# A joint product in three more pairs of units, and buffers handed out by hand, in a two-layer hybrid decoder trunk on one core

## The chip, the cores and the metric

The kernel runs on 1 core of a Trainium2 chip. The metric is the device time in microseconds; the median of 3 runs of the kernel before is 1880.92 us (1879.19 to 1881.81). Five engines work in the core, each through its own list of instructions in order: PE (TensorE) multiplies matrices into PSUM, DVE (VectorE) and ACT (ScalarE) do arithmetic on rows, POOL (GpSimd) here issues the DMAs that add into memory, and SP (SyncE) issues almost all other DMAs. 16 DMA engines carry the transfers.

## What is computed

One inference step of a decoder layer for 1024 prompt rows and 8 sample rows together (T = 1032 rows, width 1024). A projection feeds three branches: a convolution with a gated linear recurrence, windowed attention, and attention to a memory. Their results are gated, summed, projected, and normalised. Then comes the part that the change touches, the gated feed-forward block, here from the reference:

```python
h = layer_norm(ALPHA * x + merged @ w_out, ln1_g, ln1_b)
gt, up = jnp.split(h @ w_gate_up, 2, axis=-1)
h = layer_norm(ALPHA * h + (jax.nn.silu(gt) * up) @ w_down, ln2_g, ln2_b)
```

The hidden width is 2816, that is 22 blocks of 128 columns. All matrices are float32. The kernel keeps nearly full precision by writing each operand as a sum of a rounded high part and a low part (this is called a cut below: ACT copies the high part, DVE subtracts it to get the low part) and by making three matmuls per tile: high times high, high times low, low times high.

## The kernel before

**Seven products for eight.** A unit is two blocks of 128 output columns for all rows, that is a 2 x 2 arrangement of weight blocks times a 2 x 2 arrangement of row blocks. It is computed with seven block products instead of eight, numbered 0 to 6. Product i has a stationary operand made from the unit's weights (a sum or difference of quarters, `fast_quarter`, line 263 on) and a moving operand made once from the rows, `ts[p][i]`, for two quarters of the columns p = 0 and 1. One product is 2 (p) x 4 (k) x 3 = 24 matmuls of 128 x 128 by 128 x 258 (`fast_product`). `fast_step` (line 297) runs product i and then moves what is ready out of PSUM: bank b takes products 0, 2, 4 and 6 one on top of the other, so that its state must be read between them (copies p1s and u2s by ACT, the sum zb by DVE, a copy by ACT at the end); bank d takes 1 and 5; bank c takes 3. The outputs are two tiles of 128 x 1032, za and zb.

**The stages around the change.** Two gate blocks (f = 0 and 1) are made plainly. Then `gate_up_down` (line 1440) goes through a list of 28 units: 20 gate units f = 2 to 21 (gate column block f and up column block f), then 4 units of the first down part (rows of w_down for hidden blocks 0 to 7), then 4 of the second (blocks 8 to 15). The last six hidden blocks, 16 to 21, are multiplied plainly in `last_products`, where the second norm is also made. A gate unit ends in `FinishGate`: Silu of za times zb, stored to a scratch `f` in memory. A down unit ends in `FinishDown`: za and zb are added to the scratch `h` by DMAs of POOL.

**The joint product.** In the first nine pairs of gate units (u, v), the products 3 of both units use the same moving operand. They are made together with the same trick one level down (`second_quarter`, `second_step`, lines 1326 and 1350): seven half-size products called p0 (two of them), p1 (two), p4 (two) and p6 (one), 12 + 12 + 12 + 6 = 42 matmuls in place of 48. Their moving operands `t2` are made once, in `second_combos`, from tiles R of the normed rows. The tenth pair (f = 20, 21) and all down units are plain, with 7 x 24 matmuls a unit.

**The order.** The order of products is written out as a list. Three products ahead of PE the weights are cut (`quarter(*order[n + ahead])`). Side work is stepped on from the same loop: copies between memories, the means of the last weights (`weight_means`), the sums of hidden rows for the down parts (`down_sums`, which read `f`, add, and store to a scratch `t`) and the moving operands of the next part (`down_operand`: a load of 516 KB from `f` or `t` for each p, and a cut into the slots of an operand that is no longer needed). For the first down part, operand 0 is made in product 3 of the last but one gate unit, and operand i+1 in product i of the last one. A planner then puts each engine's instructions in order, by program order among those that it expects to be ready.

**Buffers.** Tiles of rows (`zt`, line 187) come from a pool of ten, sums of weights from a pool of four, raw weight tiles of 128 x 512 (256 KB) from a pool of six; the planner picks the slots. Raw weights of a unit are requested by `load` when product 1 of the unit before is issued; a pair with a joint product loads nine tiles, one of them twice.

Of the kernel before, what the change touches and what calls it, by code (L numbers as in the profile page):

```python
# [10 lines left out]
F32 = mybir.dt.float32  # L11
# [8 lines left out]
P = 128  # L20
# [40 lines left out]
class Builder:  # L61
# [124 lines left out]

    def zt(self, name):
        return self.z.tile([P, T], F32, tag="z", name=name, bufs=self.zbufs)
# [47 lines left out]
    def pair_load(self, u, st, src0, src1, other=None):  # L236

        h = D // 2
        raw = lambda j, e, src: self.half_raw(src[:, e * h:(e + 1) * h], h, f"ur{u}_{j}{e}")
        if other is not None:  # L240
            a11, a12, a21, a22 = (raw(j, e, src) for j, src in enumerate((src0, src1)) for e in range(2))
            st["second"] = raw(2, 1, other)
        else:
            a11, a21, a22, a12 = raw(0, 0, src0), raw(1, 0, src1), raw(1, 1, src1), raw(0, 1, src0)
        return {"raw": [[a11, a12], [a21, a22]], "u": u}
# [14 lines left out]

    def fast_quarter(self, st, i):

        nc, (a11, a12), u = self.nc, st["raw"][0], st["u"]
        a21, a22 = st["raw"][1] or (None, None)
        if i in (1, 2, 4, 5):
            src = st[2] if i == 5 and self.sum_bufs == 4 else self.w1.tile([P, D // 2], F32, tag="sum", name=f"us{u}_{i}",
                                                                          bufs=self.sum_bufs)
            a, b = {1: (a21, a22), 2: (st.get(1), a11), 4: (a11, a21), 5: (st.get(2), a12)}[i]
            nc.vector.tensor_add(src, a, b)
            st[i] = src  # L270
        else:
            src = {0: a11, 3: a12, 6: a22}[i]
        hi, lo = self.half_pair(f"u{u}_{i}")
        self.split(hi, lo, src)
        st["q", i] = hi, lo
# [21 lines left out]
    def fast_step(self, st, i, ts, finish):  # L297
# [9 lines left out]
        for p in range(2):  # L307
# [10 lines left out]
            if i in (0, 1, 2):  # L318
# [16 lines left out]
        if st.get("pd") is not None and i == 0:  # L335
            nc.vector.scalar_tensor_tensor(st["s", 0, 1], st["pd"]["p", 1], 1.0, st["s", 0, 1], op0=ALU.mult,
                                           op1=ALU.subtract)
# [864 lines left out]
    def out_proj(self, merged):  # L1202
        nc, io, ph = self.nc, self.io, self.ph
        h, self.R, self.norm, w = {}, {}, None, []
        for q in range(4):
            for kh in range(2):
                t = self.zt(f"R{q}{kh}")
                nc.sync.dma_start(t, io["xQ"][kh, q])
                self.R[q, kh] = t.rearrange("p (k n) -> p k n", k=4)
# [36 lines left out]
    def h_combos(self, h, ts):  # L1246
# [9 lines left out]
        for p in range(2):  # L1256
            b11, b21, b12, b22 = self.R[p, 0], self.R[p, 1], self.R[2 + p, 0], self.R[2 + p, 1]
            t1 = self.zt(f"ht1_{p}").rearrange("p (k n) -> p k n", k=4)
            tt(t1, b11, b12, ALU.subtract)
            keep(1, p, t1)  # L1260
            yield
# [6 lines left out]
            keep(6, p, b11)  # L1268
            yield

    def plain_gate_up(self, f, h, steps):
# [21 lines left out]
        nc.sync.dma_start(self.scr["f"][:, f, :], out)  # L1293

# [12 lines left out]
    def second_combos(self):  # L1307

        nc, tt = self.nc, self.nc.vector.tensor_tensor
        (b11, b21), (b12, b22) = ((self.R[p, 1][:, 0:2, :], self.R[p, 1][:, 2:4, :]) for p in range(2))  # L1310
# [12 lines left out]
        self.split(*self.t2[6], b21)  # L1323
        yield

    def second_quarter(self, su, sv, j):

        add, h = self.nc.vector.tensor_add, D // 4
        a, b = su["raw"][0][1], sv["second"]
# [4 lines left out]
        elif j == 1:  # L1334
            src, z = (self.w1.tile([P, D // 2], F32, tag="sum", name=f"us{su['u']}_p{e}", bufs=4) for e in range(2))
# [7 lines left out]
        else:  # L1343
            src, n = sv["raw"][0][1][:, hi], h
        wh, wl = self.half_pair(f"u{su['u']}_p{j}")
        self.split(wh[:, :n], wl[:, :n], src)
        for e, i in enumerate({0: (0, 3), 1: (1, 2), 4: (4, 5), 6: (6,)}[j]):
            su["w", i] = wh[:, e * h:(e + 1) * h], wl[:, e * h:(e + 1) * h]

    def second_step(self, su, sv, j, ts, fu):  # L1350

        nc, u = self.nc, su["u"]
        stt = nc.vector.scalar_tensor_tensor
        part = lambda p, e: tuple(a[:, 2 * e:2 * e + 2, :] for a in ts[p][3])
        quarter = lambda z, p: z[:, QN * p:QN * (p + 1)]
        if j == 0:
            su["p", 0], su["p", 3] = (self.bank("s", f"p{e}{u}")[:, :QN] for e in "bc")
            su["p", 1] = self.bank("o", f"pd{u}")[:, :QN]
            su["za"] = self.zt(f"za{u}")
        b, c, d = su["p", 0], su["p", 3], su["p", 1]  # L1360
        for i in {0: (0, 3), 1: (1, 2), 4: (4, 5), 6: (6,)}[j]:
# [10 lines left out]
            if i == 0:  # L1372
                stt(su["s", 0, 0], b, 1.0, su["s", 0, 0], op0=ALU.mult, op1=ALU.add)
            elif i == 3:
                stt(quarter(su["za"], 0), c, 1.0, su["s", 0, 0], op0=ALU.mult, op1=ALU.add)
# [637 lines left out]
```

## Time and profile before

| | before |
|---|---|
| median of 3 runs | 1880.92 us |
| the profiled execution | 1882.15 us |
| its span, first to last instruction | 1880.4 us |
| PE busy | 1861.4 us, 14670 matmuls |
| DVE busy | 1396.7 us, 2807 instructions |
| ACT busy | 1058.6 us, 2264 instructions |
| POOL busy | 125.0 us |
| DMA | 308.14 MB, mean 164 GB/s |
| granted PE clock, mean | 0.997 |

The stage with the list of 28 units runs from about 1237 us to about 1798 us of the span. Rows of instructions give the start, the duration, the engine, the line of the kernel, the operation, output and inputs by the program's names (`ufg_4h` is the high part of the cut weights of product 4 of a gate unit, `uf_4h` that of a down unit, `d04h` or `dth` a moving operand of a down part), and in brackets the idle time before and what ended it. A matmul's duration of 0.28 us covers its whole passage; successive ones start 0.12 us apart.

### The profile page before, as it was taken

The numbers are of one execution on the slowest core, as the hardware profiler recorded it, in microseconds if no ns is written. First come the engines' busy times: TensorE is split into PE (matmuls) and PEld (weight loads), VectorE is DVE, ScalarE is ACT, GpSimd is POOL, SyncE is SP. The second block draws the span as 40 slices with busy tenths as digits, with TensorE's granted clock in tenths as the row PEclk, the third lists the DMA queues.
The fourth block names the chain that finished last, engine by engine and source line by source line (L and its number), as shares of the span: only waits on it lengthen the run. The fifth ranks groups of instructions, "written<-read, shape, count | busy, mean of one in ns | idle before, by whom it ended". The sixth has DMA issues, their size and how long they took to land.

```text
span 1880.4 us, 37977 instructions
## 1 busy us (share of the span) xinstructions
PE 1861.4 (99%) x14670; PEld 1846.0 (98%) x14670; DVE 1396.7 (74%) x2807; ACT 1058.6 (56%) x2264; POOL 125.0 (7%) x187
## 2 busy tenths in 40 slices
PE   9999999999999999999999999999999999999998
PEld 9999999999999999999999999999999999999998
DVE  7878878888788757568787567786677667858486
ACT  6576676665666756568774234544444444635454
POOL 1001002110000000021210000000000000001100
PEclk9999999999999999999999999999999999999998
DMA  9535345447344368647535251224355345758872
GB/s 329 175 117 174 108 145 167 137 139 267 117 160 164 120 198 267 213 128 238 170 103 189 91 192 57 69 88 146 123 182 201 95 152 194 260 139 266 173 212 91
DMA packets 182213, 308.14 MB, mean 164 GB/s; under 512 B 19264, under 2 KB 97040, under 8 KB 182032
## 3 DMA queue, kind: packets, MB, share of 16 engines
q1 hardware_dynamic: 174928, 286.08, 45.9%
q0 software_dynamic: 4224, 14.78, 4.0%
q10 hardware_dynamic: 2880, 4.85, 0.7%
q8 instruction: 115, 1.88, 0.4%
q14 instruction: 66, 0.54, 0.1%
HBM read 222.10 MB, written 87.73 MB: 165 GB/s over the span
## 4 chain that ended last, share of the span: by engine, by line
PE 89%; DVE 5%; ACT 2%; DMA 2%; issue 1%; SPq 0%; POOL 0%; ACTq 0%; DVEq 0%
PE ub L285 5%; PE ub L287 5%; PE ub L286 5%; PE ubfg L286 4%; PE ubfg L287 4%; PE ubfg L285 4%; PE ud L287 2%; PE ud L286 2%; PE ud L285 2%; PE udfg L287 2%; PE udfg L285 2%; PE udfg L286 2%; PE ubf L285 2%; PE op L130 2%; PE ubf L286 2%; PE op L132 2%
## 5 line engine op out<-in xcount | busy, mean ns | idle before, releaser
L285 PE MATMUL ub<-th,u_6h 128*128 128x258 f32 x240 | 68.5, 285 | 2.7 <-DVE sq L966 1.4
L285 PE MATMUL ub<-th,u_2h 128*128 128x258 f32 x240 | 68.1, 284 | 0.7 <-ACT p1s L320 0.7
L285 PE MATMUL ub<-th,u_4h 128*128 128x258 f32 x240 | 68.2, 284 | 0.3 <-ACT u2s L320 0.3
L287 PE MATMUL ud<-th,u_5l 128*128 128x258 f32 x240 | 68.1, 284 | 0.0
L285 PE MATMUL ud<-th,u_5h 128*128 128x258 f32 x240 | 68.1, 284 | 0.0
L285 PE MATMUL ub<-th,u_0h 128*128 128x258 f32 x240 | 68.1, 284 | 0.0
L287 PE MATMUL ub<-th,u_6l 128*128 128x258 f32 x240 | 68.1, 284 | 0.0
L287 PE MATMUL ud<-th,u_1l 128*128 128x258 f32 x240 | 68.1, 284 | 0.0
L287 PE MATMUL ub<-th,u_4l 128*128 128x258 f32 x240 | 68.0, 284 | 0.0
L287 PE MATMUL ub<-th,u_2l 128*128 128x258 f32 x240 | 68.0, 284 | 0.0
L287 PE MATMUL ub<-th,u_0l 128*128 128x258 f32 x240 | 68.0, 283 | 0.0
L285 PE MATMUL uc<-th,u_3h 128*128 128x258 f32 x240 | 68.0, 283 | 0.0
L285 PE MATMUL ud<-th,u_1h 128*128 128x258 f32 x240 | 68.0, 283 | 0.0
L287 PE MATMUL uc<-th,u_3l 128*128 128x258 f32 x240 | 68.0, 283 | 0.0
L286 PE MATMUL ub<-tl,u_6h 128*128 128x258 f32 x240 | 67.7, 282 | 0.0
L286 PE MATMUL ub<-tl,u_0h 128*128 128x258 f32 x240 | 67.6, 282 | 0.0
L286 PE MATMUL ud<-tl,u_5h 128*128 128x258 f32 x240 | 67.6, 282 | 0.0
L286 PE MATMUL ud<-tl,u_1h 128*128 128x258 f32 x240 | 67.6, 282 | 0.0
L286 PE MATMUL ub<-tl,u_4h 128*128 128x258 f32 x240 | 67.6, 282 | 0.0
L286 PE MATMUL ub<-tl,u_2h 128*128 128x258 f32 x240 | 67.6, 282 | 0.0
L286 PE MATMUL uc<-tl,u_3h 128*128 128x258 f32 x240 | 67.6, 282 | 0.0
L130 PE MATMUL op<-mh,woh 128*128 128x258 f32 x224 | 63.4, 283 | 0.0
(1034 smaller groups left out, 8207.2 us busy)
## 6 DMA issues: line engine op xcount, KB each, us to landing
ur<-win SPq DMA_DIRECT2D x120, 256.0 KB, 3.4
urfg<-wgu SPq DMA_DIRECT2D x89, 256.0 KB, 3.0
scr_f<-G SPq DMA_DIRECT2D x22, 516.0 KB, 2.8
f<-scr_f SPq DMA_DIRECT2D x16, 516.0 KB, 4.0
fs<-scr_t SPq DMA_DIRECT2D x16, 516.0 KB, 5.1
dck<-cmk SPq DMA_DIRECT2D x32, 256.0 KB, 4.6
dcv<-cmvT SPq DMA_DIRECT2D x32, 256.0 KB, 4.6
urf<-wdn SPq DMA_DIRECT2D x32, 256.0 KB, 3.1
```

Of the source, the lines that this page charges most:

```text
L130: nc.tensor.matmul(ps, sh, mh, start=opens and i == 0, stop=False)
L132: self.last_mm = nc.tensor.matmul(ps, sl, mh, start=False, stop=closes and i == last).ins
L285: mm(sh[:, w], xh, start=opens and k == 0, stop=False)
L286: mm(sh[:, w], xl, start=False, stop=False)
L287: self.last_mm = mm(sl[:, w], xh, start=False, stop=k == 3).ins
```

## The change

The joint product is made in every pair but those of the second down part: in the tenth gate pair and in both pairs of the first down part as well. For that the loads, cuts and operands of a pair are rearranged, and the buffers are handed out by the program itself:

- `where`, `pairs` and `second` replace `cut`. In a pair with a joint product the order of the first unit becomes 0, 1, 2, p0, 4, p1, 5, 6 (it was 0, 1, p0, 2, 4, ...). The second unit's order stays.
- `second_step` scales by the finish's factor, since a down unit has one.
- `down_sums` for the first down part makes four more operands (tiles of 128 x 516, cut and stored to a new scratch `t2`), and `second_load` brings them back in four loads of 516 KB when p6 of the last gate pair is issued. The sums before it are reordered so that no extra tile is needed.
- `down_operand` puts operand i into the slots of operand i of the part before (`home = i`), and is called in product i of the last unit (operand 3 in p6). The homes of the last rows, last weights and the row sum are renumbered accordingly.
- Code for a joint fifth product is there (`fifth_combos`, `fifth_quarter`, `fifth_step`, `fifth_load`), but its list of pairs is empty. `fifth_combos` is still run after `second_combos`: it makes, cuts and stores four operands to a scratch `t5`.
- Eight tiles of rows stand in a queue (`zslots`); two more are added in the stage before the list and in the last stage. `zt` takes the first of the queue, `zfree` puts a tile back at its end. Four sum tiles (`sfree`) and six raw tiles (`rfree`) go the same way. Raw loads are all asked for ahead (`ask`) and issued whenever a raw tile comes free (`raw_loads`, `raw_done`). A pair loads eight tiles.
- The Silu and the product of a gate unit are written into za instead of a tile of their own.
- In the last stage the eighth tile of last weights is fetched in `last_products` instead of `last_cuts`, and rows are loaded as slots come free.

```diff
     def zt(self, name):
+        if self.zslots is not None:
+            t = self.zslots.popleft()
+            view = t[:]
+            self.zheld[id(view)] = t
+            return view
         return self.z.tile([P, T], F32, tag="z", name=name, bufs=self.zbufs)
...
+    def raw_loads(self):
+        while self.rwait and self.rfree:
+            name, st, n, src = self.rwait.popleft()
+            t = st["r"][n] = self.rfree.popleft()
+            self.last_load = self.nc.sync.dma_start(t, src).ins
+
+    def raw_done(self, st, *keys):
+        for n in keys:
+            self.rfree.append(st["r"].pop(n))
+        self.raw_loads()
...
+    def fifth_combos(self):
+        nc, tt = self.nc, self.nc.vector.tensor_tensor
+        z = [self.Rt[2 + p, 1] for p in range(2)]
+        (b11, b21), (b12, b22) = ((t[:, :2 * QN], t[:, 2 * QN:]) for t in z)
...
+        def put(j, src, sign=1.0):
+            t = self.zt(f"t5{j}")
+            pair = t.bitcast(F32R)[:, :2 * QN], t.bitcast(F32R)[:, 2 * QN:]
+            (self.split if sign > 0 else partial(self.split_scaled, scale=sign))(*pair, src)
+            nc.sync.dma_start(self.scr["t5"][:, (1, 2, 4, 6).index(j), :], t)
+            self.zfree(t)
...
+    def second_load(self, part):
+        pairs = [self.quarter_pair(q, 0, f"t2{part}") for q in (2, 3)]
+        for n, pair in enumerate(pairs):
+            for e, t in enumerate(pair):
+                self.nc.sync.dma_start(t.rearrange("p k n -> p (k n)").bitcast(F32), self.scr["t2"][:, part, n, e])
...
     def down_sums(self, part):
...
+        low = [self.down_block(part, 1, 0, p) for p in range(2)]
+        (b11, b21), (b12, b22) = ((t[:, :2 * QN], t[:, 2 * QN:]) for t in low)
+        tt(b22, b22, b12, ALU.subtract)
+        tt(b12, b11, b12, ALU.subtract)
+        yield
+        tt(b11, b22, b11, ALU.add)
+        tt(b21, b11, b21, ALU.subtract)
+        for n, pair in enumerate(((b12, b11), (b22, b21))):
...
     def down_operand(self, part, i, ts):
-        home = (i - part - 1) % 8
+        home = i
...
     def gate_up_down(self, ts):
...
-        order, cut = [], 2 * ((NF - 2 - PLAIN) // 2)
+        where = {u: n for n, u in enumerate(units)}
+        pairs = [n for n in range(0, len(units), 2) if units[n][0] != FAST - 1]
+        second = {units[n + e] for n in pairs for e in range(2)}
+        fifth = []
...
-                steps = [(u, 0), (u, 1), (u, "p0"), (u, 2), (u, 4), (u, "p1"), (u, 5), (u, 6),
+                steps = [(u, 2), (u, "p0"), (u, 4), (u, "p1"), (u, 5), (u, 6),
                          (v, 0), (v, 1), (v, "p4"), (v, 2), (v, 4), (v, "p6"), (v, 5), (v, 6)]
...
-        sums, seconds = deque(), self.second_combos()
+        sums, seconds = deque(), chain(self.second_combos([self.R[p, 1] for p in range(2)]), self.fifth_combos())
...
-                if u[1] == last[u[0]][1] - 1 and i == 3:
-                    self.down_operand(nxt, 0, moving[nxt])
-                if u == last[u[0]] and i < 6:
...
-                    self.down_operand(nxt, i + 1, moving[nxt])
+                if i == "p6":
+                    self.down_operand(nxt, 3, moving[nxt])
+                    if nxt < FAST - 1:
+                        self.second_load(nxt)
...
+                elif not isinstance(i, str):
+                    self.down_operand(nxt, i, moving[nxt])
...
-        while len(self.wraw) < KT:
+        while len(self.wraw) < KT - 1:
```

More of the change, by code (lines that the diff above doesn't have):

```diff
@@ L1504, in gate_up_down @@
             next(seconds, None)
-            if i == 6 and (where[u] >= cut or where[u] % 2):
+            if i == "v6" or i == 6 and (u not in second or where[u] % 2 and not st[u]["fifth"]):
                 del st[u]
-                if where[u] < cut:
+                if u in second:
                     del st[units[where[u] - 1]]
-            if i in (2, 5):
+            if i == 4 or i == 0 and n:
                 next(means, None)
+            if where[u] // 2 * 2 in fifth and where[u] % 2:
+                for j in {0: (1,), "p4": (2,), "v1": (4, 6)}.get(i, ()):
+                    self.fifth_load(j)
@@ L1829, in build @@
                         ts = self.plain(h)
+                        for t in more:
+                            self.zslots.remove(t)
                     with pool("w1") as self.w1:
@@ L1859, in __init__ @@
     def __init__(self, b, part, j):
-        self.b, self.rows = b, (2 * j, 2 * j + 1)
+        self.b, self.rows, self.ends = b, (2 * j, 2 * j + 1), (part, j) == (FAST - 1, 3)
     def late(self, dst, ps):
```

335 lines of the change are left out of this document (248 added, 87 removed).

## The prediction

> **What bounds the kernel now.** I read the page's busy table and its chain of waits first, then the table by stretches of time, then the order of instructions at the stages that the change touches.
>
> ```profile
> span 1880.4 us, 37977 instructions
> PE 1861.4 (99%) x14670; PEld 1846.0 (98%) x14670; DVE 1396.7 (74%) x2807; ACT 1058.6 (56%) x2264; POOL 125.0 (7%) x187
> PE 89%; DVE 5%; ACT 2%; DMA 2%; issue 1%; SPq 0%; POOL 0%; ACTq 0%; DVEq 0%
> ```
>
> PE is busy for 1861.4 of 1880.4 us and makes 89% of the chain. An average can hide a stage with another limit, so the next rows (from, to, length, then busy us and count of PE, PEld, DVE, ACT, POOL, then PE clock, DMA share, GB/s) take single stretches: an early gate pair, the last gate unit, the first down unit, and the last unit of the first down part.
>
> ```profile
> 1277.20:1317.00 39.80, 39.80 (x333) 39.80 (x332) 26.44 (x47) 16.98 (x34) 0.00 (x0) 1.00 0.36 120
> 1615.60:1635.80 20.20, 20.20 (x170) 20.20 (x170) 18.80 (x27) 16.05 (x25) 0.00 (x0) 1.00 1.00 358
> 1635.80:1656.00 20.20, 20.20 (x170) 20.20 (x170) 17.93 (x29) 10.74 (x20) 0.95 (x1) 1.00 0.41 141
> 1696.30:1716.50 20.20, 20.20 (x171) 20.20 (x170) 18.44 (x25) 15.26 (x24) 1.72 (x2) 1.00 1.02 316
> ```
>
> In all four PE has no gap and the full clock, so here a matmul less is time less. But the turns from gate to down and from the first to the second down part are tight elsewhere: DVE 18.80 and 18.44 of 20.20 us, DMA share 1.00 and 1.02. An ordinary gate pair has DVE at 26.44 of 39.80 and DMA at 0.36. So the change can win on PE and can lose only where something makes PE wait; the turns are where to look.
>
> **The change part by part. (a) Fewer matmuls.** The two products i = 3 of a pair of units (24 matmuls each, 48) become one product of a second level with 12+12+12+6 = 42. Nine gate pairs have that now; afterwards the tenth and both pairs of the first down part too: 3 x 6 = 18 matmuls less. Their price, from the chain in order of time: the first two rows are one place in two following pairs with the joint product (330 matmuls), the next two are two following plain gate units, the last two two plain down units (168 each).
>
> ```profile
> 1254.83 0.13 PE udfg L287
> ...
> 1294.56 0.13 PE udfg L287
> ...
> 1593.17 0.13 PE ubfg L286
> ...
> 1613.40 0.13 PE ubfg L286
> ...
> 1651.54 0.13 PE udf L285
> ...
> 1671.70 0.13 PE udf L285
> ```
>
> 39.73 us / 330 = 0.1204, 20.23 / 168 = 0.1204, 20.16 / 168 = 0.1200 us for one matmul. The joint product costs no more per matmul than the plain one, though its sums alternate over three banks. Saved: 6 x 0.1204 + 12 x 0.1200 = 2.16 us. [...]
>
> **(b) Work added where nothing waits.** In the new list of operands the generator for a fifth product runs although no pair uses that product (its list of pairs is empty): four sums, four cuts and four stores of 516 KB more in the first gate pair.
>
> ```profile
> 1247.09 0.69 DVE L1322 TENSOR_TENSOR R<-R 128x516 f32<-128x516 f32 x1
> 1247.69 0.69 DVE L85 TENSOR_TENSOR ufg_5l<-usfg,ufg_5h 128x512 fp32r<-128x512 f32 x1
> ...
> 1251.09 0.69 DVE L85 TENSOR_TENSOR ufg_0l<-urfg,ufg_0h 128x512 fp32r<-128x512 f32 x1 [0.17 <-PE ubfg L287]
> ...
> 1258.32 0.69 DVE L85 TENSOR_TENSOR ufg_2l<-usfg,ufg_2h 128x512 fp32r<-128x512 f32 x1 [1.93 <-PE ubfg L287]
> ...
> 1258.05 0.28 PE L285 MATMUL ubfg<-hh,ufg_0h 128*128 128x258 f32 x1
> ```
>
> Starts are 0.60 us apart: 8 x 0.60 = 4.8 us of DVE. The cover is the lead of the weight cuts: the cut ufg_0l ends at 1251.78 and PE takes it at 1258.05, 6.3 us later, and DVE waits for PE (1.93 us) soon after. I take 0; without that lead it would cost 4.8, with it in part gone at most 1. The first down part's sums get the same 8 operations at some middle gate pair, under a DVE that has 13 us idle in a pair (26.44 of 39.80): 0. The product of Silu written in place of its own tile, the scale on the joint sums, and one weight load of 256 KB less per pair (9 become 8) take nothing from or add nothing to PE's path: 0.
>
> **(c) The turn from gate to down.** Now operand i+1 of the down part is cut in step i of the last gate unit and operand 0 a unit earlier; afterwards operand i is cut in step i, all seven in one unit, into the slots just read. And that unit and the next now carry the joint product.
>
> ```profile
> 1610.85 1.24 DVE L85 TENSOR_TENSOR d00l<-f0FalseFalse,d00h 128x1032 fp32r<-128x1032 f32 x1 [0.34 <-ACT d00h L84]
> ...
> 1635.18 0.69 DVE L85 TENSOR_TENSOR uf_1l<-usf,uf_1h 128x512 fp32r<-128x512 f32 x1
> ...
> 1641.08 2.38 DVE L85 TENSOR_TENSOR d06l<-fs,d06h 128x1032 fp32r<-128x1032 f32 x2
> 1643.37 0.69 DVE L85 TENSOR_TENSOR uf_4l<-usf,uf_4h 128x512 fp32r<-128x512 f32 x1
> ...
> 1638.77 0.28 PE L285 MATMUL udf<-d01h,uf_1h 128*128 128x258 f32 x1
> ...
> 1647.40 0.28 PE L285 MATMUL ubf<-d04h,uf_4h 128*128 128x258 f32 x1
> ...
> 1653.18 0.28 PE L285 MATMUL ubf<-d06h,uf_6h 128*128 128x258 f32 x1
> ```
>
> The 6.3 us of lead are down to 1638.77 - 1635.87 = 2.9 at uf_1 and 1647.40 - 1644.06 = 3.3 at uf_4: DVE works here without idling, and its backlog is paid from the lead. The change puts into the same stretch the two cuts of operand 0 (2 x 1.15 = 2.3) and the extra DVE work of the joint product in the last gate unit (some three evacuations and half a cut, 1.05). PE reaches uf_4 sooner, too: 6 matmuls less in the gate unit (0.72), 12 less before uf_4 (1.44). 3.3 - 2.3 - 1.05 - 0.72 - 1.44 = -2.2: PE would wait 2.2 us if all cuts kept their place. If operand 6's two cuts (2.3 us, needed last) fall behind uf_4's, which its later issue allows, it waits 0. Bounds 0 to 2.2; I take 0.8, nearer the lower end: operand 6 now comes one step later in the program, so most of its cuts should fall behind uf_4's. Behind a late weight cut stands DVE's next work, the evacuations of za and zb, and the product that needs the emptied bank waits for those.
>
> At the second turn the first down part's last unit has the joint product, and the unit after it has not:
>
> ```profile
> 1722.38 0.69 DVE L85 TENSOR_TENSOR uf_4l<-usf,uf_4h 128x512 fp32r<-128x512 f32 x1
> ...
> 1728.10 0.28 PE L285 MATMUL ubf<-dth,uf_4h 128*128 128x258 f32 x1
> ```
>
> Its lead is 5.0; less 2.3, 1.05 and 0.72 leaves 0.9. Bounds 0 to 1.5; I take 0.2.
>
> **(d) Buffers by hand.** Rows and sums get eight slots in a queue instead of ten that any free one serves. A pair holds at most four, the running sums of the down operands four more: eight suffice. Weight tiles are asked for as soon as the last cut has read them; 256 KB land in 3.0 us, and a tile is freed some three steps (8 us) ahead of use. 0. Only the end differs: the last weight tile (wl7) is now fetched after the slot of wl3 is read.
>
> ```profile
> 1793.32 0.33 SPq L1600 DMA_DIRECT2D wl7r<-wdn  x1
> ...
> 1800.60 1.66 DVE L1618 SCALAR_TENSOR_TENSOR wl2l<-wl3r,wbar,wl2h 128x128 fp32r<-128x128 f32 x6
> ...
> 1806.60 1.87 ACT L1617 ACTIVATE wl6h<-wl7r,wbar 128x128 fp32r<-128x128 f32 x6
> ...
> 1812.62 0.28 PE L130 MATMUL dl<-g5h,wl6h 128*128 128x258 f32 x1
> ...
> wsum<-wdn SPq DMA_DIRECT2D x8, 384.0 KB, 4.0
> r<-scr_h SPq DMA_DIRECT2D x7, 516.0 KB, 9.3
> ```
>
> Behind a load of r, which waits for that slot (read until 1802.3), wl7 is issued near 1803 instead of 1793.32. At 4.0 us (the same size in a quiet stretch) it is cut by 1809, in time for 1812.62; at the 9.3 us of r it is cut by 1814.2 and PE waits 1.6. I take 0.1.
>
> **Sum.** -2.16 + 0 + 0.8 + 0.2 + 0.1 = -1.1 us. The profiled execution took 1882.15 us (its span 1880.4 and 1.75 around it); -1.1 makes 1881.1. It lies 1.23 above the median of the runs, 1880.92, so against that median I predict **1879.9**. About 0.2% (3.8 us) is what a measurement of this kernel can tell from no change: the three runs shown spread over 2.6.
>
> **The rivals.** *All of the gain stays*: cuts are reordered and no wait appears: 1880.92 - 2.16 = 1878.8. For it: at the first turn ACT and DVE waited for loads, and PE did not.
>
> ```profile
> ACT d00h L84 <- DMA f0FalseFalse<-scr_f: 2.5, 2, 2.1
> ...
> ACT d01h L84 <- DMA fs<-scr_t: 1.6, 1, 1.6
> ```
>
> Against it: the 2.9 us of lead left.
>
> *The loads decide at the turns, and the kernel gets slower.* In 1615.60 to 1635.80 the DMA engines are full at 358 GB/s. The change brings into this unit and the next operand 0's loads (2 x 0.53 MB) and four tiles of the joint product's down operands (4 x 0.53 MB), issued before operands 5 and 6 on the same queue: 3.2 MB / 358 GB/s = 8.9 us later landing. Operand 6 is cut by 1643.4 and used at 1653.18, 9.8 us of slack; one step later issue takes 2.9, the faster PE 2.2, so 4.7 is left against 8.9, and PE waits 4.2. At the second turn (share 1.02) operand 0's 1.06 MB at 316 GB/s are 3.4 us, of which a lead of 0.9 covers little: some 2 more. The instruction that waits is the operand's cut on ACT; behind it in ACT's order stand the high halves of the weight cuts and the copies that empty banks (p1s, u2s), and PE waits for both. 1878.8 + 6.2 = 1885. It decides as soon as landing is late by more than 4.7 us. Against it: the next unit's share of 0.41 leaves room for 12 us of transfers, and loads can start when slots are free, before the last unit. [...]
>
> *The end of the kernel decides*: wl7 late by 1.6 and another 1 to 2 us of rows waiting for slots: 1879.9 + 3 = 1883. For it: a queue hands out the longest free slot, not the one ready first; against it: two more slots are added there.
>
> *More than the matmuls is gained*: fewer waits of SP's queue make weight loads land earlier. PE has no waits there to remove, so no price below 1878.8 but by chance. That the joint product is not made in those pairs is ruled out by the list of pairs in the diff.
>
> **How the numbers follow.** Forecast with a small wait 0.42, all gain kept 0.30, loads at the turns 0.16, the end 0.08, more gained 0.04. The range reaches from 1877.6 (1878.8 less 1.2, the lowest run shown lies 1.7 below the median) to 1884.0, most of the way to the second rival. Faster by over 0.2% (below 1877.2): the 0.04 and a tenth of the 0.30 for chance, 0.07. Slower (above 1884.7): two thirds of 0.16 and some of the end, 0.14. Within: 0.79.
>
> **What would show it.** Right: PE's count falls by 18 to about 14652, pairs of the first down part take 39.6 us instead of 40.3, PE's idle time in the stretch from the tenth gate pair on is about 1 us and named after a weight cut of DVE. Wrong: PE idle behind a DMA of fs or t2 through ACT (second rival); behind wl7 (third); gaps in the first gate pair (the 4.8 us of DVE not covered); PE busy but more us per matmul.

## The result and the profile after

The kernel after took 1891.84 us (median of 4 runs, 1890.29 to 1894.14); the kernel before took 1880.06 us in the same measurement. The ratio is 1.0063 with a 95% interval of 1.0046 to 1.0081: **slower**, by 0.6% or 11.8 us in the medians (8.6 to 15.2 by the interval), where 1879.9 was forecast and 1884.0 was the end of the range. The profiled execution took 1891.85 us, its span 1890.1.

The page of the kernel after: the span, the busy time of each engine, and the chain of waits by engine.

```profile
span 1890.1 us, 38036 instructions
PE 1863.8 (99%) x14652; PEld 1846.0 (98%) x14652; DVE 1417.8 (75%) x2850; ACT 1064.0 (56%) x2278; POOL 124.1 (7%) x187
...
PE 86%; DVE 6%; DMA 4%; ACT 2%; issue 1%; POOL 0%; SPq 0%; ACTq 0%; DVEq 0%
```

The 18 matmuls are gone (14652 instead of 14670), yet PE's busy time rose by 2.4 us, and the chain has 4% of DMA instead of 2%. Fewer matmuls took longer in sum. The table by stretches shows where. First the kernel before, then the kernel after; the columns are those of the prediction's table.

```profile
1236.00:1282.00 46.00, 46.00 (x382) 45.90 (x381) 37.56 (x69) 22.52 (x45) 0.00 (x0) 1.00 0.40 134
...
1640.00:1680.00 40.00, 40.00 (x336) 40.00 (x335) 24.71 (x42) 15.70 (x34) 3.59 (x4) 1.00 0.48 114
1680.00:1720.00 40.00, 40.00 (x335) 40.00 (x335) 30.38 (x44) 25.65 (x43) 3.06 (x4) 1.00 0.94 296
1720.00:1760.00 40.00, 40.00 (x335) 40.00 (x334) 22.73 (x39) 14.36 (x32) 7.19 (x9) 1.00 0.70 150
```

```profile
1236.00:1282.00 46.00, 43.09 (x344) 42.58 (x344) 40.27 (x75) 22.85 (x45) 0.00 (x0) 0.96 0.49 164
...
1640.00:1680.00 40.00, 37.24 (x305) 36.41 (x303) 27.64 (x47) 20.71 (x38) 1.83 (x2) 1.00 0.71 202
1680.00:1720.00 40.00, 37.41 (x309) 37.20 (x310) 28.99 (x49) 21.01 (x39) 3.50 (x4) 1.00 0.74 192
1720.00:1760.00 40.00, 39.28 (x327) 39.07 (x326) 27.99 (x45) 19.31 (x37) 5.01 (x6) 1.00 0.86 228
```

Count the matmuls that each stretch did not get done: 382 - 344 = 38 in the first gate pair, then 336 - 305 = 31, 335 - 309 = 26 and 335 - 327 = 8 from the first turn on, 103 together. At 0.1204 us each that is 12.4 us; less the 2.16 saved it is 10.2. From its first matmul (1237.06 instead of 1237.61) to the first of the last stage (1807.28 instead of 1797.45) the list of units took 570.2 us instead of 559.8, 10.4 more; it begins 0.55 us sooner, and the two spans differ by 9.7. The 358 us between, from 1282 to 1640, hold 2971 matmuls instead of 2976. So to within some half a microsecond the account closes with two places: **the first gate pair (4.6 us) and the stretch from the first turn to the second (7.8 us)**. Between the two PE has no gap. Of the 7.8 us, 6.1 are idle time (40 less PE's busy 37.24, 37.41 and 39.28). Each of the five waits there costs some 0.26 us more than its idle time: nothing overlaps the last matmul before it, which counts 0.28 us instead of 0.12, and the matmul right behind it is followed after 0.22 us instead of 0.12 (1715.92 and 1716.14, for one). That places 1.3 us of the rest.

PE's waits from 1235 to 1810 us in the kernel after (what was waited for: us in total, times, longest) and the first that waited, with its start and, in brackets, the idle time before it:

```profile
PE ubf L328 <- ACT u2sf L367: 3.0, 2, 2.5
PE udfg L328 <- ACT ufg_1h L84: 2.7, 1, 2.7
PE pbf L1526 <- DVE p1sf L1530: 1.3, 1, 1.3
PE ubf L328 <- DVE z L374: 0.9, 1, 0.9
PE ubf L328 <- ACT z L2091: 0.7, 1, 0.7
```

```profile
1242.76 0.39 PE L328 MATMUL udfg<-hth,ufg_1h 128*128 128x258 f32 x1 [2.65 <-ACT ufg_1h L84]
```

**First gate pair.** PE finished product 0 and stood for 2.65 us until the second product's weights were cut. Behind the wait the granted clock was 0.57 (1.00 in the kernel before), and successive matmuls started 0.21 us apart instead of 0.12 (1244.72, 1244.94 and 1245.15, for three), which is a part of the rise in busy time: 3 us of the kernel before, and the same 3 us of the kernel after.

```profile
1244.00:1247.00 3.00, 3.00 (x28) 3.00 (x27) 3.00 (x8) 1.22 (x5) 0.00 (x0) 1.00 0.88 274
```

```profile
1244.00:1247.00 3.00, 3.00 (x15) 3.00 (x16) 3.00 (x8) 1.48 (x4) 0.00 (x0) 0.57 0.53 161
```

15 matmuls instead of 28 in the same 3 us of "busy" PE, at a clock of 0.57. The sum of two weight tiles from which product 1's cut is made comes first on the path. It was at 1239.04 before and is at 1241.37 after; ahead of it now stand operations that nothing waits for yet (L1394 belongs to the unused fifth product).

```profile
1239.04 0.69 DVE L269 TENSOR_TENSOR usfg<-urfg,urfg 128x512 f32<-128x512 f32 x1
```

```profile
1238.94 0.69 DVE L1394 TENSOR_TENSOR z<-z,z 128x516 f32<-128x516 f32 x1
...
1241.37 1.28 DVE L302 TENSOR_TENSOR s<-raw,raw 128x512 f32<-128x512 f32 x2
```

**Second turn.** PE's longest wait here, 2.46 us, stands behind ACT, and ACT behind the load of operand 3:

```profile
1714.53 1.05 ACT L84 CAST d13h<-z 128x1032 fp32r<-128x1032 f32 x1 [3.06 <-DMA z<-scr_f]
...
1715.92 0.39 PE L328 MATMUL ubf<-dth,uf_4h 128*128 128x258 f32 x1 [2.46 <-ACT u2sf L367]
```

SP issued that load at 1710.21, after a wait of 2.7 us for the accumulating store of 1704.64. The chain of waits of the kernel after goes through the next such store, to the wait of 0.72 us behind it:

```profile
1712.88 8.43 DMA scr_h<-z
1721.32 4.96 DMA z<-scr_f
1726.31 1.05 ACT d13h L84
1727.36 0.29 ACT z L2091
```

Each load of operand 3 waits for its row tile, which the store of a down unit's sums (scr_h<-z) still reads; ACT waits in order for that load, and behind it stand the copies that empty PE's banks. SP's waits for such stores between 1640 and 1760 us:

```profile
SPq L1610 <- DMA scr_h<-z: 14.5, 2, 8.1
...
SPq L1549 <- DMA scr_h<-z: 5.0, 2, 2.7
```

The kernel before has no wait of SP for scr_h in that stretch. The transfers as such were not fuller than before: by the tables above their share from 1680 to 1760 us is 0.80 on average, against 0.82. The first of these rows also explains the middle of the first down part: a raw weight load stood in SP's order behind an operand load that waited, and DVE idled 7.24 us for it.

```profile
1678.25 0.42 DVE L1488 TENSOR_TENSOR s<-raw 128x256 f32<-128x256 f32 x1 [7.24 <-DMA raw<-wdn]
```

The last stage did not change: from its first matmul to the end of the span it is 1890.1 - 1807.28 = 82.8 us, against 1880.4 - 1797.45 = 82.9.

```profile
1807.28 0.28 PE L130 MATMUL dl<-g7h,wl0h 128*128 128x258 f32 x1
```

### The profile page after: what moved, and what is told of

It is laid out like the page before. It is cut to its first block, busy times and chain, and to the rows that moved or that the text cites. A ratio compares the mean times of both kernels' runs of the same rounds, so it can differ in the third digit from the quotient of the medians.

```text
span 1890.1 us, 38036 instructions
## 1 busy us (share of the span) xinstructions
PE 1863.8 (99%) x14652; PEld 1846.0 (98%) x14652; DVE 1417.8 (75%) x2850; ACT 1064.0 (56%) x2278; POOL 124.1 (7%) x187
## 4 chain that ended last, share of the span: by engine, by line
PE 86%; DVE 6%; DMA 4%; ACT 2%; issue 1%; POOL 0%; SPq 0%; ACTq 0%; DVEq 0%
PE ub L328 5%; PE ub L330 5%; PE ub L329 5%; PE ubfg L328 4%; PE ubfg L329 4%; PE ubfg L330 4%; PE ud L330 2%; PE ud L329 2%; PE ud L328 2%; PE udfg L330 2%; PE udfg L328 2%; PE udfg L329 2%; PE op L130 2%; PE op L132 2%; PE op L131 2%; PE brs L141 2%
## 5 line engine op out<-in xcount | busy, mean ns | idle before, releaser
L2095 POOL DMA_DIRECT2D scr_h<-z x16 | 14.5, 1001 | 749.4 <-DVE uf_2l L85 669.7
```

What stands on the lines that cost most here:

```text
L2095: self.b.nc.gpsimd.dma_start(self.b.scr["h"][:, m, :], z, accum_op=ALU.add)
```

## The experiments

Three readings stood against each other at the first gate pair and the two turns: the added work (of DVE in the first pair, of the joint product in the down part), the tiles handed out by hand, and the transfers' bytes. Each run is named by what it changes against the kernel after.

**no_fifth: the unused product's operands left out.**

```diff
-        sums, seconds = deque(), chain(self.second_combos(...), self.fifth_combos())
+        sums, seconds = deque(), self.second_combos(...)
```

> The kernel after without the four operands of the unused fifth product (8 operations of DVE and four stores of 516 KB less in and ahead of the first gate pair). Theory *extra work*: these operations stand ahead of the first weight sum and cause PE's wait of 2.65 us and the slow clock behind it; without them the first pair takes 39.7 us again instead of 44.5, in all 1891.8 - 4.5 = 1887.3. Theory *the row tile*: the first sum tile lies where one of the two extra row tiles lay, and that one is still read by the store of the last plain unit (issued at 1237.84, some 2.6 us to land, so free at about 1240.5); the sum can't start before, whatever else DVE does. Then the wait of PE at the second product stays above 2 us and the time is 1891.4, at most 0.6 below 1891.8.

1891.13 us (ratio 1.006, 1.0043 to 1.0076). The extra work is not the cause: with it gone PE still waits at the same place.

```profile
1239.35 0.39 PE L328 MATMUL udfg<-hth,ufg_1h 128*128 128x258 f32 x1 [2.45 <-ACT ufg_1h L84]
```

Other operations took the free places in DVE's order ahead of the sum. So something else holds the sum back, and the planner fills the time.

**g_slot: the last plain unit's output into another row tile.** The same work; the tile is not one of the two that are lent out before the list of units.

```diff
     def zt(self, name):
+            if name == f"G{PLAIN - 1}":
+                # rotate the queue to the first tile that is not lent out
...
```

> The kernel after, but the output of the last plain unit is put into one of the eight row tiles and not into one of the two that give their room to the sum tiles; the work is the same, the fifth product's operands included. Theory *the row tile*: the first sum starts some 2 us sooner (by its place among DVE's instructions, one short operation behind the last cut instead of five), PE's wait falls from 2.65 to under 0.8 us and the clock stays at 1.00: 1891.8 - 4.2 = 1887.6. Theory *extra work*: the same number of operations stands in DVE's queue, so nothing changes: 1891.8.

1889.73 us (ratio 1.0046, 1.0029 to 1.0062; 4 runs from 1884.66 to 1891.23). The same kernel beside a later experiment:

> The same kernel as the run that moved the last plain unit's output, beside the plain store on the same chip, since its four times lay 6.6 us apart: 1889.0, and its waits as there.

1886.05 us (9 runs, ratio 1.0029, 1.0019 to 1.0039). In both, the first gate pair has no wait of PE left and the clock is 1.00; g_slot_again:

```profile
1236.00:1282.00 46.00, 45.82 (x378) 45.40 (x378) 41.18 (x76) 23.97 (x49) 0.00 (x0) 1.00 0.54 188
```

378 matmuls instead of 344, 34 x 0.1204 = 4.1 us, with all the fifth product's operations in place (DVE 41.18 us busy). So the theory of the row tile holds: the first sum tile's room was last used by a row tile that the store of the last plain unit was still reading. That store is issued at 1237.84, and its packets ran until about 1240.1; the sum began at 1241.37, 3.5 us behind the issue.

```profile
1237.84 0.33 SPq L1344 DMA_DIRECT2D scr_f<-z  x1
```

**ten_slots: ten row tiles throughout, none lent out.**

```diff
-    self.zslots = deque(... for i in range(8))
+    self.zslots = deque(... for i in range(10))
-    more = self.more_slots(self.ph)
```

> The kernel after with ten row tiles throughout instead of eight and two lent out at both ends. Theory *slots*: it removes the wait of the first sum (4.3 us, as moving the output does) and most of the waits of the operands' loads for tiles that an accumulating store still reads: the wait of the raw load in the middle of the first down part (0.9) and at the second turn (about 3.0) go, the first turn keeps its 2.4: 1891.8 - 4.3 - 3.5 = 1884.0. Rival *full DMA and DVE at the turns*: the waits at the second turn stay, as the loads only move: 1891.8 - 4.3 = 1887.5. If the extra work is the cause in the first pair, that part of the gain is missing too: 1888.3 with the slots, 1891.8 without.

1887.74 us (1.0038, 1.0023 to 1.0053). The first pair is cured here too (PE waits 0.29 us). The second turn is not, against the theory and as its rival had it (1887.5): one load still stood 6.9 us behind an accumulating store, and PE's wait there grew to 4.4 us.

```profile
PE ubf L328 <- ACT z L2087: 4.4, 1, 4.4
```

```profile
SPq L1549 <- DMA scr_h<-z: 9.6, 2, 6.9
```

Two tiles more in one queue do not keep a load away from a tile in use; they only change which load meets it. But PE's 4.4 us are not shown to come from that: ACT had idled 6.34 us for a load until 1717.23, and the load that stood behind the store was issued only at 1716.96. The load that ACT waited for was issued by 1708.1, and from 1707 to 1717 us the transfers' share was 1.01.

**gates_only: the joint product in the ten gate pairs alone.** The sums and loads of its operands for the down part go with it.

```diff
-        pairs = [n for n in range(0, len(units), 2) if units[n][0] != FAST - 1]
+        pairs = [n for n in range(0, len(units), 2) if units[n][0] == "g"]
```

> The kernel after with the joint product in the ten gate pairs alone: both pairs of the first down part are made plain, and the four operands for them (a sum of 8 operations, four stores and four loads of 516 KB) are left out. 12 matmuls come back (1.44 us). If the waits from the first turn to the second (together about 6.3 us) come from the joint product's extra work and loads, they go: 1891.8 + 1.4 - 6.3 = 1886.9. If the eight slots cause those of the middle and of the second turn (3.9 us), only the first turn's 2.4 us go: 1891.8 + 1.4 - 2.4 = 1890.8.

1885.53 us (1.0031, 1.0018 to 1.0044). From the first turn to the end of the list no wait of PE is left, with the eight tiles. What is left in the whole list is the first pair's, this row and 0.4 us behind it:

```profile
PE udfg L328 <- ACT ufg_1h L84: 2.7, 1, 2.7
```

So without the joint product in the down part these waits are gone (gates_g below, the same with the last plain unit's output in another tile, keeps 1.28 us). That does not clear the tiles yet: both may be needed.

**g_plain_store: the sums stored without accumulating.** On top of g_slot; the instructions of all engines stand in the same order in both kernels.

```diff
-            self.b.nc.gpsimd.dma_start(self.b.scr["h"][:, m, :], z, accum_op=ALU.add)
+            self.b.nc.gpsimd.dma_start(self.b.scr["h"][:, m, :], z)
```

> The kernel with the last plain unit's output moved (1889.7), and each down unit's sums are stored to scr_h by a plain store instead of an accumulating one. The adding up of the two down parts and the residual is left out with it; every instruction of every engine stands in the same order as before, and the bytes are the same but for what the accumulating reads. Theory *the slow store holds the tile*: an accumulating store of 516 KB took 6.3 us (median, first down part), a plain one of the same size 2.6 to 2.8; with the plain one the operands' loads start some 3.5 us sooner each, SP's waits for scr_h<-z fall from 14.5 + 13.1 us to under 5, and PE's waits at the second turn (2.2 + 1.4) and in the middle (0.7) fall to under 1 together: 1889.7 - 3.5 = 1886.2. Rival *joint product's work*: the order and the work are the same, so the waits stay: 1889.7.

1882.91 us (1.0013, 1.0004 to 1.0023), against 1886.05 of g_slot_again on the same chip: 3.1 us for the accumulating alone. Between 1640 and 1740 us the store's median from issue to landing fell from 6.3 to 3.7 us, and the longest wait of PE at the second turn from 3.73 to 0.34 us. First g_slot_again, then g_plain_store:

```profile
scr_h<-z POOLq DMA_DIRECT2D x8, 516.0 KB, 6.3
...
1711.29 0.58 PE L330 MATMUL ubf<-dth,uf_4h 128*128 128x258 f32 x1 [3.73 <-ACT u2sf L369]
```

```profile
scr_h<-z POOLq DMA_DIRECT2D x9, 516.0 KB, 3.7
...
1718.80 0.39 PE L330 MATMUL ubf<-d10h,uf_0h 128*128 128x258 f32 x1 [0.34 <-ACT z L2093]
```

So the accumulating store is a cause at the second turn, and with gates_only the joint product, which has used up the lead, is the other; either without the other leaves PE there between 0 and 1.28 us. How the store acts is in part argued. SP's waits for it fell (from 14.9 and 4.1 us to 8.3 and 3.0), and in the kernel after and g_slot_again a load of the second turn was issued only after 2.7 us of such a wait. But the plain store also takes less of the transfers' time (its queue's share in that stretch fell from 26.7% to 12.3%, for 4.76 MB in either run), and raw weight loads landed in 2.6 us instead of 4.4. No run holds the tile as long and leaves the transfers free.

**g_sorted, ten_sorted: tiles that a store has read go to the next sums only.** The sums za and zb take from that list first; loads of operands never meet an accumulating store then.

```diff
-            self.b.zfree(za, zb)
+            for z in (za, zb):
+                self.b.zlate.append(self.b.zheld.pop(id(z)))
```

> The kernel of the run that moved the last plain unit's output (1889.7), and the row tiles that an accumulating store of a down unit has read go back to a list of their own, from which only the sums za and zb of later units are served; loads of operands take the other tiles. No load of an operand waits for an accumulating store then; work and bytes are the same. Theory *slots*: SP's queue waits no more for scr_h<-z, the raw load in the middle of the first down part (0.7 us of PE) and the operands d13 and d15 at the second turn (2.2 + 1.4 us of PE) come in time: 1889.7 - 3.9 = 1885.8 to 1886.5. Rival *joint product's work*: the operand cuts, joint cuts and loads are simply too much for DVE, ACT and the transfers at the second turn, whichever tiles they take: 1889.7, with the waits still there.

1885.89 us (10 runs, 1.0028, 1.0019 to 1.0038), the expected time, but not as expected, and no gain beside the 1886.05 of g_slot_again. SP's waits for scr_h are gone, and the evacuations that write the sums wait for the stores instead. PE stood 2.95 us behind one of them at 1717.26. DVE's row between 1640 and 1760 us:

```profile
DVE z L377 <- DMA scr_h<-z: 10.0, 3, 5.9
```

> Ten row tiles throughout (1887.7) and the list of their own for tiles that an accumulating store has read. Theory *slots*: with ten tiles in one queue PE still waited 4.4 us at the second turn, because one load of an operand stood 6.9 us behind an accumulating store; that goes, with the slow clock behind it: 1887.7 - 4.8 = 1882.9, and what is left over the gain of 2.16 us is the first turn. Rival *joint product's work*: 1887.7.

1889.84 us (1.005, 1.0035 to 1.0065): worse than ten_slots, and the theory's 1882.9 was wrong. The sorting makes waits of this kind itself (1.12 us at 1714.97, behind a sum that waited for a store). The longest, 3.03 us at 1738.45, is another: it lies in the second down part, behind a raw weight load that took 8.4 us while the transfers' share was 1.03.

**ten_defer_no_fifth: such tiles go back to the common queue one down unit later.**

```diff
-            self.b.zfree(za, zb)
+            self.b.zlate.append((za, zb))
+            if len(self.b.zlate) > 1:
+                self.b.zfree(*self.b.zlate.popleft())
```

> The joint product in all pairs as in the kernel after, with ten row tiles, without the operands of the unused fifth product, and a tile that an accumulating store has read goes back to the common queue one down unit (20 us) later. Loads of operands and sums then take tiles whose store has long landed, at the price that fewer tiles go round. Theory *slots*: PE's waits in the middle and at the second turn go below 1 us, the first turn keeps 1 to 2 us: 1880.8 - 2.2 + 1.5 + 0.7 = 1880.8, with no difference from before. Rival *joint product's work*: some 4 us of waits stay at the second turn: 1885.

1884.92 us (1.003, 1.002 to 1.004). A miss, and the time of the rival (1885): SP still waited for stores. PE's 2.07 us at the second turn, though, stand behind a load of 7.7 us, issued at 1711.81 while the transfers' share was 1.04, and not behind a store. No order of ten tiles that I tried removes the wait.

**gates_g, gates_ten, gates_ten_no_fifth: the part of the change without its waits.** The joint product in the gate pairs alone, with the last plain unit's output moved (gates_g), or with ten tiles (gates_ten), or with ten tiles and without the fifth product's operands.

> The joint product in the ten gate pairs alone (1885.5), and the last plain unit's output in one of the eight tiles. If the waits are all named (first gate pair: the row tile; all others: the first down part with its joint products), no wait of PE is left between the first gate unit and the end, and 6 matmuls (0.72 us) are saved against the kernel before: 1880.9 - 0.7 = 1880.2. If something else in the buffers handed out by hand costs time, it is above 1881.5.

1882.62 us (10 runs, 1.0009, 1.0000 to 1.0018), above the 1881.5 that was to show something else in the buffers: with eight tiles a wait of 1.28 us stays at the second turn. SP waits 4.2 us for such a store with an operand's load, and the load that PE then waits behind took 8.1 us in full transfers (share 1.06 from 1707 to 1715 us).

> The joint product in the ten gate pairs alone, ten row tiles, and the fifth product's operands made as in the kernel after (the run without them had 1879.97). If they are covered by the lead of the weight cuts once the first weight sum doesn't wait for the row tile, the time is the same within 0.5: 1880.2; if the first pair has no cover for 4.8 us of DVE, PE waits there and it is 1882 or more.

1879.98 us (10 runs, 1.0003, 0.9993 to 1.0012; the kernel before had 1879.54 there).

> The joint product in the ten gate pairs alone, ten row tiles throughout, and without the operands of the unused fifth product. Theories agree on no wait of PE from the first gate unit to the end: 1880.2. Against the run with the moved output it shows what the fifth product's operands still cost where they are covered: 0 if the cover of the weight cuts' lead is whole (then both are equal within 0.5), up to 0.5 if not.

1879.97 us (10 runs, 0.9995, 0.9985 to 1.0005).

> The kernel with the joint product in the ten gate pairs alone, ten row tiles and without the fifth product's operands, which had 1879.97 against 1880.75 of the kernel before: 6 matmuls less (0.72 us) and no wait of PE to pay for them. If that is all there is, it is 0.7 faster than before and the interval of the ratio lies about 0.9996, too near 1 to tell apart; if the ordering by hand costs something elsewhere, it is at 1 or above.

1879.44 us against 1880.51 (11 runs, 0.9995, 0.9986 to 1.0004). In two measurements it is 0.8 and 1.1 us below the kernel before, about the 0.72 that 6 matmuls are worth, but both intervals reach over 1: it is the best kernel of this study, and not shown to be faster. With and without the fifth product's operands the first pair's stretch has nearly the same count of matmuls, so these 4.8 us of DVE cost nothing that can be seen once the sum does not wait. First gates_ten, then gates_ten_no_fifth_again:

```profile
1236.00:1282.00 46.00, 45.70 (x379) 45.49 (x379) 41.81 (x75) 24.58 (x50) 0.00 (x0) 1.00 0.55 188
```

```profile
1236.00:1282.00 46.00, 45.84 (x381) 45.63 (x380) 37.03 (x68) 21.86 (x45) 0.00 (x0) 1.00 0.42 136
```

**g_no_t2_load: the joint product's operands not loaded at the first turn.** On top of g_slot.

```diff
-                    if nxt < FAST - 1:
-                        self.second_load(nxt)
```

> The kernel with the last plain unit's output moved (1886.0 beside the plain store), without the four loads of the joint product's down operands (2.1 MB) at the first turn; the joint product of the first down part reads the gate stage's operands instead, so its sums are not the reference's, and nothing else is left out. At the first turn DVE idled 1.20 and 1.49 us behind ACT's d03, which waited 1.1 and 1.3 us for its load, and PE then waited 1.5 to 2.2 us. Theory *loads*: 2.1 MB at 358 GB/s are 5.9 us less for the transfers; ACT's waits for d03 and d05 go, DVE has 2.7 us more, and PE's waits between 1640 and 1660 fall below 0.5 us: 1886.0 - 1.6 = 1884.4, with the second turn as it was. Theory *DVE's work*: the two cuts of operand 0 and the extra evacuations are the cause; PE still waits some 1.5 us there: 1886.0.

1889.41 us (1.0046, 1.003 to 1.0061). With 2.1 MB less in the transfers PE still waits 0.48 + 0.91 + 0.21 = 1.6 us at the first turn, as long as in g_slot_again (0.18 + 1.34).

```profile
1646.10 0.39 PE L1530 MATMUL pbf<-d03h,uf_p0l 128*128 128x258 f32 x1 [0.48 <-DVE uf_p0l L85]
...
1648.49 0.39 PE L330 MATMUL ubf<-dth,uf_4h 128*128 128x258 f32 x1 [0.91 <-ACT uf_4h L84]
...
1649.45 0.39 PE L332 MATMUL ubf<-dth,uf_4l 128*128 128x258 f32 x1 [0.21 <-DVE uf_4l L85]
```

So the bytes of these loads are not what keeps PE there. The test is not quite clean: the planner put a cut of operand 5 ahead of those of operand 3 in this run, and the waits stand at other products. The second turn was about as late as in g_slot_again (3.42 us against 3.73), and the whole was not faster.

**first_pair: the joint product in the gate pairs and the first pair of the first down part.** With ten tiles and without the fifth product's operands.

```diff
+        pairs = [... if units[n][0] == "g" or units[n] == (0, 0)]
```

> Ten row tiles, no operands of the unused fifth product, the joint product in the ten gate pairs and in the first of the two pairs of the first down part (the second pair made plain): 12 matmuls less than before (1.44 us). The run without the four loads left PE's waits at the first turn (0.48 + 0.91 + 0.21 us), so bytes are not their cause. Theory *DVE's work in the first down unit*: four short sums of 0.34 us each, one more cut of 0.60 and the evacuations of the joint banks come on top of the operands' cuts in a stretch in which DVE has no idle time; PE waits 1.1 to 1.6 us between 1640 and 1660 as in the ten-tile run with all pairs, and nothing at the second turn: 1879.7 - 0.7 + 1.4 = 1880.4. If the first turn's wait came from the second pair or from the buffers, it is gone: 1879.0. If the second turn's wait doesn't need the joint product in its own unit, 2 to 4 us stay there: 1883.

1881.73 us (10 runs, 1.001, 1.0001 to 1.002). At the first turn PE waits 0.36 + 0.94 + 0.21 = 1.5 us, at the second none, though SP still waits for the stores there:

```profile
PE ubf L328 <- ACT uf_4h L84: 0.9, 1, 0.9
PE pbf L1528 <- DVE uf_p0l L85: 0.4, 1, 0.4
PE ubf L330 <- DVE uf_4l L85: 0.2, 1, 0.2
```

```profile
SPq L1549 <- DMA scr_h<-z: 6.3, 2, 3.2
```

So the first turn's wait belongs to the joint product in the first pair of the down part and the second turn's to that in the second pair. The first pair gains 6 x 0.12 = 0.72 us and pays 1.5 and more: the time is 1.3 us above the 1880.4 expected, and that rest is not placed.

## Why the prediction was wrong

**(a) Fewer matmuls: right, as far as it goes.** 18 are gone, each worth 0.1204 us in the account above that closes with the spans, and where PE has no gap a matmul takes what it took (358 us / 2971 = 0.1205 from 1282 to 1640 us, 358 / 2976 = 0.1203 before); it was longer behind the wait of 2.65 us, at a clock of 0.57. The gain of the tenth gate pair is in agreement with the 0.8 to 1.1 us of gates_ten_no_fifth, but not shown by them; the down part's gain of 1.44 was never seen alone.

**(b) The added work in the first gate pair: right at 0, by the wrong rows.** The 4.8 us of DVE cost nothing (gates_ten). But the lead of 6.3 us was read at the second unit's product 0, and the first unit's product 1 has no such lead: its sum was at 1239.04, its cut at 1240.85, and PE came to product 1 at 1240.49 and took the low half at 1241.59, right behind the cut. The sign "gaps in the first gate pair (the 4.8 us of DVE not covered)" did appear, with another cause.

**(d) Buffers by hand: this is the step that failed.** It counted the tiles that are needed at one time ("eight suffice") and put 0. A count says nothing on *when* a tile comes free. It cost about 4.1 us in the first pair, where the two lent tiles went to the sum tiles with a store still running on one (2.65 us of waiting and 15 instead of 28 matmuls in the next 3 us), and 3.1 us at the second turn and the middle of the part, where loads met accumulating stores (g_plain_store; a part of the 3.1 may be the transfers' time that the accumulating takes). The observation that would have given it stood in the prediction, used for the end only: "a queue hands out the longest free slot, not the one ready first".

**(c) The turns: the first was mis-sized.** 0.8 us was taken, with a bound of 2.2. The waits of the kernel after are 0.59 and 1.33 us, 1.92 together. The sum counted the joint product's DVE work in the last gate unit and left out that of the down unit behind it. DVE in the kernel after has no idle time from 1644.28 until behind the last row here, and these rows stand ahead of the evacuation on which the joint product waits:

```profile
1644.28 1.23 DVE L85 TENSOR_TENSOR d03l<-z,d03h 128x1032 fp32r<-128x1032 f32 x1 [1.49 <-ACT d03h L84]
...
1651.92 0.42 DVE L1490 TENSOR_TENSOR s<-raw,raw 128x256 f32<-128x256 f32 x1
...
1655.54 0.42 DVE L1530 SCALAR_TENSOR_TENSOR p1sf<-pbf,p1sf 128x258 f32<-128x258 f32 x1
```

Four short sums like the one shown, 0.34 us each, and a cut of 0.60 are 2 us of DVE work that the sum did not contain. That this work is what PE waits for is argued from the rows and from first_pair; no run took away these operations alone. The 1.49 us in which DVE waited for operand 3 belong to it too, and why that load is late there (a tile held by a gate unit's store, for one) was not tested by itself. The second turn was put at 0.2 with a bound of 1.5; PE waited 2.46 + 0.72 = 3.2, by the store of (d), which the bound did not contain.

**The rivals.** *The loads decide at the turns* (1885) had the place and the path right: the operand's cut waits on ACT, behind it stand the copies that empty banks. Its mechanism, full transfers, is not what the kernel after shows: at the first turn g_no_t2_load kept the waits without the bytes, and at the second the loads were issued late, with the transfers no fuller than before. It has a part in other runs (ten_slots, ten_defer_no_fifth, gates_g), where PE waited behind loads of 7.7 us and more. Its price did not hold the first gate pair. *The end decides*: the last stage is 82.8 us, as before, so late rows and wl7 cost nothing. *All gain stays* needs no waits; only the gate-pair variants come near it.

## What to carry to other kernels

When buffers are handed out by hand, look for each tile's last reader and how long it takes, transfers above all, and ask what is given that memory next; a count of tiles in use shows neither. Here a tile that a store of 6.3 us was reading cost on a load (SP waited 14.9 and 4.1 us in g_slot_again) or on a sum (DVE waited 10.0 us in g_sorted), whichever asked next; where the work behind it had lead enough, it cost nothing that can be seen (in gates_ten SP waited 10.2 and 6.8 us with operands' loads, and PE not at all from the first turn on). The lead that hides work has to be read at the product where the work is added, not at the next one like it.

## What the runs showed of the hardware

**An accumulating store of 516 KB took 7.7 us, a plain one 3.1.** In the kernel after, by the page's list of transfers, medians from issue to landing:

```profile
scr_f<-z SPq DMA_DIRECT2D x22, 516.0 KB, 3.1
...
scr_h<-z POOLq DMA_DIRECT2D x16, 516.0 KB, 7.7
```

The queues differ too (SP, POOL), but with the queue and the order kept, g_plain_store's 3.7 us against 6.3 from 1640 to 1740 us puts 2.6 us on the accumulating.

**The granted clock fell after waits of PE of 2.07 to 3.73 us, and not after one of 2.46.** In 3 us close behind the wait it was 0.57 after 2.65 us (the kernel after, first gate pair), 0.50 after 3.73 us (g_slot_again), 0.70 after 2.07 us (ten_defer_no_fifth), but 1.00 after 2.46 us (the kernel after, second turn):

```profile
1711.00:1714.00 3.00, 2.71 (x12) 2.71 (x13) 2.96 (x3) 2.94 (x5) 0.00 (x0) 0.50 1.04 233
```

```profile
1721.00:1724.00 3.00, 3.00 (x18) 3.00 (x19) 3.00 (x4) 2.69 (x5) 0.88 (x1) 0.70 1.00 244
```

```profile
1716.00:1719.00 3.00, 3.00 (x25) 3.00 (x26) 3.00 (x5) 3.00 (x5) 0.00 (x0) 1.00 1.03 269
```

A wait of PE could so cost more than its length: 12 matmuls in the 2.71 us that PE was busy in the first of these rows, where 0.1204 us each would make 22.5, are another 1.3 us (an estimate from these numbers). The length of the wait alone does not tell whether the clock falls: after 2.07 us it was 0.70, after 2.46 us 1.00. What decides, these runs do not show.
